# A hybrid encoder step on one core: mixer pairs interleaved over four PSUM banks, weight parts traced ahead, element-wise steps moved to ScalarE

## The chip, the core and the metric

The kernel runs on one core of a Trainium2 chip. The metric is device microseconds of one execution: 2014.56 us before the change, the median of three runs (2006.13 to 2015.11). Engines are named as the profile names them: PE is the matmul engine TensorE (PEld its weight loads), DVE is VectorE, ACT is ScalarE, POOL is GpSimd, and SP is the engine that issues most transfers.

## What is computed

One layer of a streaming encoder is applied to 576 tokens (512 of a prompt, 64 of a sample with caches), with 1024 channels, all in fp32:

- x + 1/2 SwiGLU(RMSNorm(x)), with a hidden width of 4096;
- plus a mixer: one input projection of RMSNorm(x) feeds three branches. Branch A is a Mamba-2 SSD scan (16 heads of 64, 4 groups, state 128, causal convolution of width 4, SiLU gate). Branch B is attention over a band of chunks (8 heads of 64, softmax with a bias by relative distance). Branch C is an mLSTM (4 heads of 128, exponential input gate, running maximum). Each branch is projected to 1024 channels, multiplied by a sigmoid gate of its own, summed, and projected again;
- plus a second half SwiGLU, and a final RMSNorm.

The outputs are the two results and the new states and caches.

## The kernel before

**Stages.** In order of time: the first SwiGLU (to about 595 us of the span), the plain products for the mixer's first two units (to 643), the mixer's pairs with the branches between them (643 to 1250), the merge of the branches with the output projection (its last matmul starts at 1422), the second SwiGLU and the final norm. Tokens lie on the free axis, channels on the 128 partitions.

**Split products.** Each fp32 weight tile is split into a high part `ph` (a cast on ACT, L268) and a low part `pl` (a subtraction on DVE, L269), and so are the activations (TH and TL). A product sums three matmuls per 128 rows, hi x hi, hi x lo and lo x hi (`product`, L563): 4 x 3 = 12 matmuls of 288 columns each.

**Seven products for eight.** Two output tiles of 128 channels are made together, as a 2 x 2 block product with seven sub-products, Winograd's form of Strassen's scheme. The seven are named X1 to X4, A11, A21, A22 after the weight block they take. X1 is the sum of two blocks, added up by an accumulating transfer from POOL (L445) into the tile `wx` (x12, which also holds X2). X3 and X4 are sums that POOL makes (`wy`, L456). In the mixer one such pair of output tiles is a call of `pair` (L466): it fetches the next pair's weights, splits all seven weight blocks of this pair behind the evacuations of the middle of the pair before it (`self.middle`, an `issue_after`), and issues the products in the order X1, X4, X2 of the pair before, X3, A21, A11, A22. Intermediate sums are copied from PSUM to `uv` tiles (L485, on ACT), and results leave through `emit` (L491 on ACT, L493 on DVE).

**PSUM.** Eight banks: in the mixer three for `acc`, two each for the tags `s` and `x`, one for `v`. A pair takes three `acc` banks, and the next pair starts one bank further on. `x` holds transpositions on PE (L769, L772, L814, L985, L1083, L1087), and in the mLSTM and SSD jobs one accumulation.

**Units and jobs.** The mixer works through twelve units: a0 to a3 (two attention heads each), m0 to m3 (one mLSTM head each), s0 to s3 (one SSD group each), in the order `a0 a1 m0 s0 a2 a3 s1 m1 s2 m2 s3 m3`. A unit's input tiles come from pairs (those of a0 and a1 from plain products ahead of the pairs), and then its job (`attn`, `ml`, `ssd`) is queued. A job is a Python generator: every product calls `tick` (L529), and each tick lets the first job of the queue trace its next step, or counts down a gap that the step asked for. Jobs run strictly one after another. Gate pairs (`merge_gates`, 12 in all) make the tanh inputs of the merge gates and store them to DRAM (`gs`). There are 23 unit pairs and 12 gate pairs, 35 x 7 = 245 products. After each unit's pairs comes one gate pair, and then the unit's job is queued. The last two units have two gate pairs each.

**Buffers.** Rings of tiles by tag: `g` 9, `t` 5, `P` 4, `uv` 3 in the mixer; `wr` 5, `wx` 2, `wy` 2, `ph` 6, `pl` 6 for weights. The tag `P` serves the attention scores (L834, L852), the mLSTM's decay matrix and the raw input of the SSD convolution (L1004).

**What sets the order.** A planner orders the instructions of every engine at build time: it prefers what was traced earlier, among what a simulated run of the program finds ready. The engines then run their queues strictly in that order.

## Time and profile before

| What | Value |
|---|---|
| Median of three runs | 2014.56 us (2006.13 to 2015.11) |
| The profiled execution | 2008.22 us, its span 2006.5 us |
| Mean granted TensorE clock | 0.981 |
| PE busy | 1938.0 us, 97% of the span |
| PE weight loads | 1868.3 us, 93% |
| DVE busy | 1376.9 us, 69% |
| ACT busy | 987.8 us, 49% |
| POOL busy | 637.0 us, 32% |

How to read the views. Groups of instructions: source line, engine, operation, output<-inputs, shape, count | busy us in total, mean ns of one | idle us of the engine just before them, and what ended it. Stretches: from:to, length, busy us (and count) of PE, PEld, DVE, ACT and POOL, then the granted clock, the busy share of the DMA engines and GB/s. Waits: who waited for whom, us in total, how many, the longest. Order of time: start, duration, engine, line, operation, and in brackets the idle time before it. A tile's name is the program's own, and a line can be that of a helper.

### The profile page before, as it was taken

The page shows a single profiled execution, that of the slowest core. Times are in us where ns is not written, and L with a number is a line of the kernel's source. Part 1 is how long each engine was busy: PE and PEld are TensorE (multiplying, and loading weights), DVE is VectorE, ACT ScalarE, POOL GpSimd, SP SyncE. Part 2 cuts the span into 40 slices and gives each one's busy share as a digit, 9 for nine tenths or more (in the row PEclk, how much of TensorE's full clock was granted, in tenths as well). Part 3 has the DMA queues.
Part 4 walks back from the last instruction along what each step waited for, and adds up shares of the span by engine and source line. Part 5 has one row for each costly group of instructions (what it writes and reads, how often), then busy time and mean ns, then how long its engine had stood idle before and what let it go on. Part 6 is the DMA issues. An engine that isn't in the chain of part 4 may idle for free. (4 is left out here: it accounts for less than half of the span.)

```text
span 2006.5 us, 37549 instructions
## 1 busy us (share of the span) xinstructions
PE 1938.0 (97%) x14177; PEld 1868.3 (93%) x14177; DVE 1376.9 (69%) x2475; ACT 987.8 (49%) x2153; POOL 637.0 (32%) x626
## 2 busy tenths in 40 slices
PE   9899999999999999998999898899999999999998
PEld 8899999999999768877888888899999999999998
DVE  8866656666678958777686766665786665666565
ACT  4545434534544556666574754333554443454454
POOL 5223313322202326423534354351142322223221
PEclk9899999999999979999999999899999999999999
DMA  6346445544643436753655567652234644464441
GB/s 195 82 129 165 120 127 148 144 116 125 166 135 102 137 98 152 206 149 95 189 149 166 157 167 209 223 173 80 79 110 122 158 133 121 131 164 121 122 117 63
DMA packets 126622, 278.18 MB, mean 139 GB/s; under 512 B 14032, under 2 KB 25936, under 8 KB 126440
## 3 DMA queue, kind: packets, MB, share of 16 engines
q1 hardware_dynamic: 100648, 201.74, 30.3%
q0 software_dynamic: 16304, 59.52, 16.4%
q10 hardware_dynamic: 9488, 14.52, 2.4%
q8 instruction: 112, 1.84, 0.4%
q14 instruction: 70, 0.57, 0.1%
HBM read 255.16 MB, written 20.56 MB: 137 GB/s over the span
## 5 line engine op out<-in xcount | busy, mean ns | idle before, releaser
L570 PE MATMUL acc<-TH,ph 128*128 128x288 f32 x2548 | 769.4, 302 | 15.6 <-ACT uv L485 5.2
L570 PE MATMUL acc<-TL,ph 128*128 128x288 f32 x2548 | 758.6, 298 | 3.4 <-DVE TL L269 3.4
L570 PE MATMUL acc<-TH,pl 128*128 128x288 f32 x2548 | 757.4, 298 | 2.1 <-DVE pl L269 2.0
L268 ACT CAST ph<-wr 128x512 fp32r<-128x512 f32 x495 | 306.0, 620 | 481.0 <-PE acc L570 209.1
L570 PEld LDWEIGHTS acc<-TH,ph 128*128 128x128 f32 x2548 | 481.8, 189 | 27.7 <-ACT uv L485 7.4
L570 PEld LDWEIGHTS acc<-TH,pl 128*128 128x128 f32 x2548 | 483.0, 190 | 8.6 <-issue 4.7
L570 PEld LDWEIGHTS acc<-TL,ph 128*128 128x128 f32 x2548 | 482.5, 189 | 6.8 <-DVE TL L269 3.6
L269 DVE TENSOR_TENSOR pl<-wr,ph 128x512 fp32r<-128x512 f32 x495 | 378.2, 766 | 125.1 <-ACT ph L268 115.6
L240 PE MATMUL acc<-YH,ph 128*128 128x320 f32 (+1 forms) x1536 | 453.3, 297 | 6.4 <-DVE y L1214 3.2
L240 PE MATMUL acc<-YL,ph 128*128 128x320 f32 (+1 forms) x1536 | 455.1, 297 | 2.6 <-DVE YL L319 2.1
L240 PE MATMUL acc<-YH,pl 128*128 128x320 f32 (+1 forms) x1536 | 452.3, 296 | 0.0
L240 PEld LDWEIGHTS acc<-YH,ph 128*128 128x128 f32 x1536 | 291.0, 190 | 7.8 <-DVE y L1214 3.7
L240 PEld LDWEIGHTS acc<-YL,ph 128*128 128x128 f32 x1536 | 292.1, 190 | 4.3 <-DVE YL L319 3.5
L240 PEld LDWEIGHTS acc<-YH,pl 128*128 128x128 f32 x1536 | 291.3, 190 | 0.0
L456 POOL TENSOR_TENSOR wy<-wx,wr 128x512 f32<-128x512 f32 x91 | 133.0, 1462 | 442.3 <-DVE pl L269 191.1
L445 POOL DMA_DIRECT2D wx<-in_sblk x91 | 80.6, 889 | 374.9 <-DMA wx<-in_sblk 165.0
L269 DVE TENSOR_TENSOR pl<-wx,ph 128x512 fp32r<-128x512 f32 x182 | 171.3, 941 | 36.3 <-ACT ph L268 33.5
L269 DVE TENSOR_TENSOR pl<-wy,ph 128x512 fp32r<-128x512 f32 x182 | 149.3, 830 | 50.5 <-ACT ph L268 50.4
L631 DVE SCALAR_TENSOR_TENSOR R<-acc,R 128x256 f32<-128x256 f32 (+1 forms) x256 | 116.1, 454 | 90.2 <-PE acc L240 86.9
L268 ACT CAST ph<-wy 128x512 fp32r<-128x512 f32 x182 | 112.4, 621 | 100.2 <-PE acc L240 63.0
L268 ACT CAST ph<-wx 128x512 fp32r<-128x512 f32 x182 | 112.7, 619 | 94.8 <-PE acc L570 63.3
L456 POOL TENSOR_TENSOR wy<-wy,wr 128x512 f32<-128x512 f32 x91 | 135.3, 1486 | 32.3 <-DMA wr<-in_sblk 16.2
(290 smaller groups left out, 2216.5 us busy)
## 6 DMA issues: line engine op xcount, KB each, us to landing
wr<-in_sblk SPq DMA_DIRECT2D x273, 256.0 KB, 2.8
wr<-in_wblk SPq DMA_DIRECT2D x222, 256.0 KB, 3.1
wx<-in_sblk SPq DMA_DIRECT2D x91, 512.0 KB, 4.0
wx<-in_sblk POOLq DMA_DIRECT2D x91, 512.0 KB, 5.7
gs<-g SPq DMA_DIRECT2D x24, 288.0 KB, 3.4
R<-scr_rows ACTq DMA_DIRECT2D x12, 576.0 KB, 5.6
y<-gs POOLq DMA_DIRECT2D x24, 288.0 KB, 3.5
y<-ys POOLq DMA_DIRECT2D x16, 288.0 KB, 3.6
```

What stands on the lines that cost most here:

```text
L240: nc.tensor.matmul(ps[:, :n], wt[:, wsl], xx[:, k0 + k, a:a + n], start=(k == 0 and i == 0), stop=(k == nk - 1 and i == 2))
L268: self.nc.scalar.copy(hi, src)
L269: self.nc.vector.tensor_tensor(lo, src, hi.bitcast(F32), op=ALU.subtract)
L445: nc.gpsimd.dma_start(x12, src[:, 1:3, :], accum_op=ALU.add)
L456: self.nc.gpsimd.tensor_tensor(o, one, two, op=ALU.add)
L570: self.nc.tensor.matmul(ps, wt[:, wsl], xx[:, kk, :], start=(start and kk == 0 and i == 0), stop=(kk == 3 and i == 2), skip_group_check=True)
L631: nc.vector.scalar_tensor_tensor(x[:, ot, sl], ps, 0.5, x[:, ot, sl], op0=ALU.mult, op1=ALU.add)
```

## The change

Five things change.

1. `pair` becomes `pairs`, which walks one list of products for the whole mixer. A round of pair n is X1(n), A22(n-1), X4(n), A11(n), X3(n), X2(n-1), A21(n), so that two pairs are always open. The banks are fixed: `acc0` and `acc3` in turn for the products that share a bank (X1, X3, A22, X2), `acc1` for X4 and A21, `acc2` for A11. There are four `acc` banks, and `x` has one bank instead of two.
2. A weight block's parts are no longer made for a whole pair at once: the parts of product i + 5 are traced ahead of product i. The `issue_after` on the middle of the pair is gone. `wx` has three buffers, `uv` four.
3. Three element-wise steps go to ACT: the softmax rescale (from DVE), the weighted values `wv` of the mLSTM (from POOL), and the weighted inputs `xw` of the SSD (two instructions on POOL become ten on ACT).
4. A unit's job is queued when X2 of its last pair has been issued, ahead of the gate pair and no longer behind it. The unit before last has no gate pair, and four gate pairs come after the last unit.
5. To make room, a pad is smaller, and the descriptor scratch of the transfers that POOL issues is 8192 bytes. The feed-forward units call the same `operand`, so that their two POOL additions are traced after two of the parts.

```diff
@@ -39,10 +40,13 @@
 FBUFS = {"P": 6, "g": 4}
-WBUFS = {"wr": 5, "wx": 2, "wy": 2, "ph": 6, "pl": 6}
+WBUFS = {"wr": 5, "wx": 3, "wy": 2, "ph": 6, "pl": 6}
 PAD = 2700
-PBUFS = {"s": 2, "x": 2, "v": 1}
+PBUFS = {"s": 2, "x": 1, "v": 1}
 NWARM = 14
+
+AHEAD = 5
+NGATES = {10: 0, 11: 4}
@@ -168,11 +171,8 @@
-    def pair_banks(self):
-
-        got = [self.bank()[:, :FH] for _ in range(3)]
-        self.bank_i += self.pair_step - 3
-        return got
+    def half_bank(self, i):
+        return self.acc.tile([128, 512], F32, name="acc", tag=f"acc{i}", bufs=1)[:, :FH]
@@ -449,7 +445,7 @@
-    def stationary(self, raw):
+    def operand(self, raw, t):
@@ -457,32 +453,34 @@
         x12 = raw["x12"]
-        x3 = add(x12[:, 0, :], raw[2])
-        x4 = add(x3, raw[3])
-        at = {self.T_X1: x12[:, 0, :], self.T_X2: x12[:, 1, :], self.T_X3: x3, self.T_X4: x4,
-              self.T_A11: raw[0], self.T_A22: raw[2], self.T_A21: raw[3]}
-        return {t: self.parts(at[t]) for t in (self.MUSE if self.mixer else self.FUSE)}
-
-    def pair(self, one, two, nxt):
-
-
-
-
-        nc = self.nc
-        ((name, c1), s1, put1), ((_, c2), s2, put2) = one, two
-        raw = self.fetched
-        if nxt:
-            self.fetched = self.fetch(nxt)
-        with ExitStack() as order:
-            for i in self.middle:
-                order.enter_context(self.tc.issue_after(i))
-            ops = self.stationary(raw)
-        pa, pc, pb = self.pair_banks()
+        if t in (self.T_X3, self.T_X4) and "x3" not in raw:
+            raw["x3"] = add(x12[:, 0, :], raw[2])
+            raw["x4"] = add(raw["x3"], raw[3])
+        return self.parts({self.T_X1: x12[:, 0, :], self.T_X2: x12[:, 1, :], self.T_X3: raw.get("x3"),
+                           self.T_X4: raw.get("x4"), self.T_A11: raw[0], self.T_A22: raw[2], self.T_A21: raw[3]}[t])
+
+    def pairs(self, seq):
+
+
+
+
+        nc = self.nc
+        uses = [(n - d, t) for n in range(len(seq) + 1) for d, t in (
+            (0, self.T_X1), (1, self.T_A22), (0, self.T_X4), (0, self.T_A11), (0, self.T_X3), (1, self.T_X2), (0, self.T_A21))
+            if 0 <= n - d < len(seq)]
+        raw, ops, st = {}, {}, {}
         H = (slice(0, FH), slice(FH, T))
+        def make(n, t):
+            for m in (n, n + 1):
+                if m < len(seq) and m not in raw:
+                    (((name, c1), _, _), ((_, c2), _, _)), _ = seq[m]
+                    raw[m] = self.fetch((name, c1, c2))
+            ops[n, t] = self.operand(raw[n], t)
+
         def tmp(ps, scale):
-            o = self.gp.tile([128, FH], F32, name="uv", tag="uv", bufs=3)
-            self.last = nc.scalar.activation(o, ps, AF.Copy, scale=scale).ins
+            o = self.gp.tile([128, FH], F32, name="uv", tag="uv", bufs=4)
+            nc.scalar.activation(o, ps, AF.Copy, scale=scale)
             return o
@@ -490,38 +488,42 @@
                     return
-                self.last = nc.vector.scalar_tensor_tensor(dst, ps[:, a:b], scale, other[:, a:b], op0=ALU.mult,
-                                                           op1=op).ins
+                nc.vector.scalar_tensor_tensor(dst, ps[:, a:b], scale, other[:, a:b], op0=ALU.mult, op1=op)
                 if func:
...
-        self.product(pa, ops, self.T_X1, True)
-        v = tmp(pa, s1)
-        self.product(pc, ops, self.T_X4, True)
-        m6 = tmp(pc, s2)
-        self.pair_end()
-        self.product(pa, ops, self.T_X3, False)
-        u = tmp(pa, s2)
-        self.middle = [self.last]
-        self.product(pc, ops, self.T_A21, False)
-        put2(1, H[1], emit(pc, s2, u, ALU.subtract))
-        self.middle.append(self.last)
-        self.product(pb, ops, self.T_A11, True)
-        put1(1, H[1], emit(pb, s1, v, ALU.add))
-        self.product(pa, ops, self.T_A22, False)
-        put2(0, H[0], emit(pa, -s2, m6, ALU.add))
-
-        def end():
-            self.product(pa, ops, self.T_X2, False)
-            put1(0, H[0], emit(pa, s1))
-        self.open_pair = end
-
-    def pair_end(self):
-
-        end, self.open_pair = self.open_pair, None
-        if end:
-            end()
+        for i, (n, t) in enumerate(uses):
+            for u in uses[(i + AHEAD if i else 0):i + AHEAD + 1]:
+                make(*u)
+            ((_, s1, put1), (_, s2, put2)), done = seq[n]
+            o = st.setdefault(n, {})
+            if t == self.T_X1:
+                o["a"] = self.half_bank(3 * (n % 2))
+            elif t == self.T_X4:
+                o["c"] = self.half_bank(1)
+            elif t == self.T_A11:
+                o["b"] = self.half_bank(2)
+            bank = {self.T_X4: "c", self.T_A21: "c", self.T_A11: "b"}.get(t, "a")
+            ps = o[bank]
+            self.product(ps, ops.pop((n, t)), t, t in (self.T_X1, self.T_X4, self.T_A11))
+            if t == self.T_X1:
+                o["v"] = tmp(ps, s1)
+            elif t == self.T_X4:
+                o["m6"] = tmp(ps, s2)
+            elif t == self.T_A11:
+                put1(1, H[1], emit(ps, s1, o["v"], ALU.add))
+            elif t == self.T_X3:
+                o["u"] = tmp(ps, s2)
+            elif t == self.T_A21:
+                put2(1, H[1], emit(ps, s2, o["u"], ALU.subtract))
+            elif t == self.T_A22:
+                put2(0, H[0], emit(ps, -s2, o["m6"], ALU.add))
+            else:
+                put1(0, H[0], emit(ps, s1))
+                if done:
+                    done()
+                del raw[n], st[n]
@@ -562,7 +564,7 @@
         self.tick()
-        hi, lo = ops[t]
+        hi, lo = ops
         th, tl = self.T[t]
@@ -573,31 +575,34 @@
         nc = self.nc
-        ops = self.stationary(self.fetch(desc))
-        pa, pb, pc = self.pair_banks()
+        raw = self.fetch(desc)
+
+        ops = {t: self.operand(raw, t) for t in (self.T_X1, self.T_A11, self.T_X3, self.T_X4, self.T_A22, self.T_A21,
+                                                 self.T_X2)}
+        pa, pb, pc = (self.bank()[:, :FH] for _ in range(3))
         e = lambda: self.P((128, FH))
         g = self.wp.tile([128, 2, FH], F32, name="g", tag="g", bufs=FBUFS["g"])
-        self.product(pa, ops, self.T_X1, True)
+        self.product(pa, ops[self.T_X1], self.T_X1, True)
...
@@ -802,7 +807,7 @@
             nc.vector.reciprocal(r[:, 0:1], total)
-            nc.vector.tensor_scalar(P[:, :nk], P[:, :nk], r[:, 0:1], None, op0=ALU.mult)
+            nc.scalar.activation(P[:, :nk], P[:, :nk], AF.Copy, scale=r[:, 0:1])
@@ -939,7 +944,7 @@
             wv = self.unit([128, 130], "wv", 2)
-            nc.gpsimd.tensor_scalar(wv[:n, :129], v1[:n, c, :], wc[:n, c:c + 1], 1.0, op0=ALU.mult, op1=ALU.mult)
+            nc.scalar.activation(wv[:n, :129], v1[:n, c, :], AF.Copy, scale=wc[:n, c:c + 1])
             pc = self.ps("s")
@@ -1087,10 +1092,10 @@
                                     self.TM[:64, 4:5, d0:d0 + 2].unsqueeze(3).broadcast_to([64, 1, 2, 64]), op=ALU.mult)
-            nc.gpsimd.tensor_tensor(h4(xw[:, 0:4, :]), h4(xd[:, 0:4, :]),
-                                    wd[:, 0:4, :].unsqueeze(3).broadcast_to([128, 4, 2, 64]), op=ALU.mult)
-            nc.gpsimd.tensor_tensor(h4(xw[:64, 4:5, :]), h4(xd[:64, 4:5, :]),
-                                    wd[:64, 4:5, :].unsqueeze(3).broadcast_to([64, 1, 2, 64]), op=ALU.mult)
+            for c, (a, n) in enumerate(CH):
+                for r in range(2):
+                    hs = slice(r * 64, (r + 1) * 64)
+                    nc.scalar.activation(xw[:n, c, hs], xd[:n, c, hs], AF.Copy, scale=wd[:n, c, r:r + 1])
@@ -1294,7 +1299,7 @@
             self.pbufs = PBUFS
-            self.banks, self.bank_i, self.pair_step = 3, 0, 1
+            self.banks, self.bank_i = 4, 0
             self.mixer = True
@@ -1316,7 +1321,7 @@
         with self.pools("m0", op=None, xp=None):
-            self.op.tile([128, 84], F32, name="pad")
+            self.op.tile([128, 8], F32, name="pad")
             self.XH, self.XL = self.pair_of(self.xp, [128, 8, T], ("XH", "XL"))
@@ -1335,12 +1340,15 @@
             self.ss = [na[:, a:a + n] for a, n in HALVES]
-            queue = lambda n: self.jobs.append(units[ORDER[n][0]][1](ORDER[n][1], got[ORDER[n]][1]))
+            def queue(n):
+                self.jobs.append(units[ORDER[n][0]][1](ORDER[n][1], got[ORDER[n]][1]))
+                if n == len(ORDER) - 2:
+                    self.jobs.append(self.ssd_norm())
             queue(0)
...
             self.side = self.gates(pre)
-
             seq = []
+            gates = iter(range(12))
             for n in range(2, len(ORDER)):
@@ -1350,18 +1358,9 @@
                 seq += [(tiles[j:j + 2], None) for j in range(0, len(tiles), 2)]
-                seq.append((self.merge_gates(n - 2), n))
-                if n - 2 >= len(ORDER) - 4:
-                    seq.append((self.merge_gates(n), None))
-            descs = [(one[0][0], one[0][1], two[0][1]) for (one, two), _ in seq] + [None]
-            self.fetched = self.fetch(descs[0])
-            for (tiles, n), nxt in zip(seq, descs[1:]):
-                self.pair(*tiles, nxt)
-                if n is not None:
-                    queue(n)
-                    if n == len(ORDER) - 2:
-                        self.jobs.append(self.ssd_norm())
-            self.pair_end()
+                seq[-1] = (seq[-1][0], partial(queue, n))
+                seq += [(self.merge_gates(next(gates)), None) for _ in range(NGATES.get(n, 1))]
+            self.pairs(seq)
             self.drain()
@@ -1446,7 +1445,7 @@
-    nc = bacc.Bacc("TRN2", target_bir_lowering=False, num_devices=1)
+    nc = bacc.Bacc("TRN2", target_bir_lowering=False, num_devices=1, dynamic_dma_scratch_size=8192)
     I = {k: nc.dram_tensor("in_" + k, s, F32, kind="ExternalInput").ap() for k, s in _INS.items()}
```

More of the change, by code (lines that the diff above doesn't have):

```diff
@@ L16 @@
 from contextlib import ExitStack, contextmanager, nullcontext
+from functools import partial
 import numpy as np
@@ L83, in __init__ @@
         self.b_i = 0
-        self.open_pair, self.middle = None, ()
         self.jobs, self.gap, self.side = deque(), 0, iter(())
@@ L130, in ffn_phase @@
             self.pbufs = {"x": 2}
-            self.banks, self.bank_i, self.pair_step = 6, 0, 3
+            self.banks, self.bank_i = 6, 0
             self.mixer = False
@@ L430 @@
     T_X3, T_A11, T_A21, T_X2, T_A22, T_X4, T_X1 = range(7)
-    FUSE = (T_X1, T_A11, T_X3, T_X4, T_A22, T_A21, T_X2)
-    MUSE = (T_X1, T_X4, T_X3, T_A21, T_A11, T_A22, T_X2)
     def fetch(self, desc):
@@ L575, in swiglu_unit @@
         nc = self.nc
-        ops = self.stationary(self.fetch(desc))
-        pa, pb, pc = self.pair_banks()
+        raw = self.fetch(desc)
+        ops = {t: self.operand(raw, t) for t in (self.T_X1, self.T_A11, self.T_X3, self.T_X4, self.T_A22, self.T_A21,
+                                                 self.T_X2)}
+        pa, pb, pc = (self.bank()[:, :FH] for _ in range(3))
         e = lambda: self.P((128, FH))
         g = self.wp.tile([128, 2, FH], F32, name="g", tag="g", bufs=FBUFS["g"])
-        self.product(pa, ops, self.T_X1, True)
+        self.product(pa, ops[self.T_X1], self.T_X1, True)
         v = e()
         nc.scalar.copy(v, pa)
-        self.product(pb, ops, self.T_A11, True)
+        self.product(pb, ops[self.T_A11], self.T_A11, True)
         nc.vector.tensor_tensor(g[:, 1, :], pb, v, op=ALU.add)
-        self.product(pa, ops, self.T_X3, False)
+        self.product(pa, ops[self.T_X3], self.T_X3, False)
         u = e()
         nc.scalar.copy(u, pa)
-        self.product(pc, ops, self.T_X4, True)
+        self.product(pc, ops[self.T_X4], self.T_X4, True)
         m6 = e()
         nc.scalar.copy(m6, pc)
-        self.product(pa, ops, self.T_A22, False)
+        self.product(pa, ops[self.T_A22], self.T_A22, False)
         s0 = e()
@@ L594, in swiglu_unit @@
         nc.scalar.activation(s0, s0, AF.Silu)
-        self.product(pc, ops, self.T_A21, False)
+        self.product(pc, ops[self.T_A21], self.T_A21, False)
         s1 = e()
@@ L599, in swiglu_unit @@
         nc.gpsimd.tensor_tensor(g[:, 1, :], g[:, 1, :], s1, op=ALU.mult)
-        self.product(pa, ops, self.T_X2, False)
+        self.product(pa, ops[self.T_X2], self.T_X2, False)
         nc.vector.tensor_tensor(g[:, 0, :], pa, s0, op=ALU.mult)
```

## The prediction

> **What bounds it now.** I read the engine totals first, then the engines by stretch, then the matmul engine's waits inside the mixer, then the order of time around the one long hole.
>
> ```profile
> span 2006.5 us, 37549 instructions
> PE 1938.0 (97%) x14177; PEld 1868.3 (93%) x14177; DVE 1376.9 (69%) x2475; ACT 987.8 (49%) x2153; POOL 637.0 (32%) x626
> ```
>
> The matmul engine (PE) is busy 97% of the span, so it sets the end, and only its idle time and its slow stretches can be won. The next view gives busy us of PE, weight load, VectorE, ScalarE and GpSimd by stretch, with the granted clock.
>
> ```profile
> 100.00:150.00 50.00, 50.00 (x378) 50.00 (x377) 31.27 (x53) 20.70 (x40) 13.12 (x11) 1.00 0.46 127
> 655.00:700.00 45.00, 42.72 (x271) 35.33 (x272) 44.61 (x100) 23.23 (x61) 12.97 (x12) 0.96 0.47 130
> 740.00:1000.00 260.00, 247.60 (x1803) 220.46 (x1802) 196.11 (x391) 159.44 (x412) 117.01 (x117) 0.99 0.58 156
> 1000.00:1247.00 247.00, 228.53 (x1650) 215.14 (x1649) 177.14 (x326) 148.36 (x381) 111.01 (x115) 0.97 0.60 166
> 1247.00:1296.00 49.00, 39.26 (x272) 37.53 (x271) 29.07 (x58) 16.99 (x39) 14.71 (x26) 0.93 0.74 235
> 1296.00:1480.00 184.00, 183.52 (x1364) 182.63 (x1363) 123.80 (x225) 75.81 (x146) 62.90 (x64) 0.99 0.33 105
> ```
>
> The feed-forward stretch at 100 runs without a hole: 50/378 = 0.132 us a matmul, 1.59 us a product of 12, 11.1 us a pair of 84. So the feed-forward parts have nothing to give, and their edits (a third wx buffer, the two GpSimd additions traced after two parts instead of ahead of all) count nothing: full PE work hides them, and if that cover failed, the cost would be about one GpSimd addition a unit (1.46 us, its row stands below). All the loss lies between 655 and 1296. These waits end inside the mixer's pairs (745 to 1250; us in total, times, longest) and, below the dots, at the step into the merge (1247 to 1300):
>
> ```profile
> PE ps_s L1117 <- POOL t L1090: 8.4, 3, 3.4
> PE ps_s L944 <- POOL wv L942: 5.2, 4, 2.0
> PE acc L570 <- ACT uv L485: 5.2, 7, 1.5
> PE acc L570 <- DVE pl L269: 2.0, 2, 1.2
> PE acc L570 <- DVE R L493: 1.9, 1, 1.9
> PE acc L570 <- DVE g L493: 1.6, 3, 0.8
> PE acc L570 <- DVE P L493: 1.3, 1, 1.3
> ...
> PE ps_x L955 <- DMA cs<-in_mc: 3.4, 1, 3.4
> PE acc L240 <- DVE y L1214: 3.2, 1, 3.2
> PE acc L240 <- ACT YH L268: 2.5, 1, 2.5
> ```
>
> The named waits in the pairs come to 25.6 us. One hole is larger and shows in no row of waits. In order of time, PE and then VectorE, with the stretch's totals:
>
> ```profile
> 707.96 0.29 PE L570 MATMUL acc<-TH,pl 128*128 128x288 f32 x1
> ...
> 738.86 0.40 PE L570 MATMUL acc<-TH,ph 128*128 128x288 f32 x1
> ...
> 737.50 0.16 DVE L851 TENSOR_TENSOR sm<-sm 128x1 f32<-128x1 f32 x1
> 737.58 0.88 DVE L493 SCALAR_TENSOR_TENSOR P<-acc,uv 128x224 f32<-128x224 f32 x3
> ...
> 708.10:738.80 30.70, 27.06 (x110) 13.63 (x107) 14.42 (x53) 16.51 (x59) 0.49 (x5) 0.61 0.29 78
> ```
>
> For 30.9 us no product runs. PE does one attention job alone, at a granted clock of 0.61. It ends when VectorE empties a bank into a P tile, right behind the job's last softmax step. The first SSD unit's convolution input and the attention scores share the four P buffers, and the job's last P is traced first.
>
> **The change, part by part.** Base: the profiled execution's 2008.2 us (span 2006.5 and 1.7 around it). The three timed runs have a median of 2014.56, from 2006.13 to 2015.11, so the base lies at their lower end.
>
> ```profile
> L1090 POOL TENSOR_TENSOR t<-t,wd 128x512 f32<-128x512 f32 x8 | 9.8, 1223 | 7.4 <-DVE t L1084 7.4
> L1092 POOL TENSOR_TENSOR t<-t,wd 64x128 f32<-64x128 f32 x8 | 7.7, 965 | 1.9 <-DVE t L1088 1.5 <-ACT sq L279 0.4
> L456 POOL TENSOR_TENSOR wy<-wx,wr 128x512 f32<-128x512 f32 x91 | 133.0, 1462 | 442.3 <-DVE pl L269 191.1 <-DMA wx<-in_sblk 93.4 <-DMA wr<-in_sblk 52.5
> L853 ACT ACTIVATE P<-ps_s,sm 128x64 f32<-128x64 f32 x4 | 1.2, 308 | 0.0
> L942 POOL TENSOR_SCALAR wv<-t,wc 128x129 f32<-128x129 f32 (+1 forms) x20 | 11.2, 620 | 12.6 <-ACT t L770 10.0 <-PE ps_s L944 2.6
> L1099 ACT ACTIVATE R<-R,TM 128x128 f32<-128x128 f32 (+1 forms) x80 | 25.4, 381 | 0.0
> L805 DVE TENSOR_SCALAR P<-P,sm 128x128 f32<-128x128 f32 (+4 forms) x36 | 15.8, 439 | 0.3
> L834 ACT ACTIVATE P<-ps_s,sm 128x128 f32<-128x128 f32 (+3 forms) x32 | 16.8, 525 | 7.2 <-DVE P L805 3.3 <-DVE sm L833 2.2 <-DVE TM L739 1.6
> L485 ACT ACTIVATE uv<-acc 128x288 f32<-128x288 f32 x105 | 42.4, 406 | 39.6 <-PE acc L570 34.2 <-DVE g L1021 3.9 <-DMA scr_rows<-R 1.4
> ```
>
> *xw to ScalarE.* Eight times, 1.22 + 0.97 = 2.2 us on GpSimd become ten activations 64 wide, 3.1 us at 0.308 each. But the first chunk is ready after two of them (0.6 us), and it no longer queues behind a 1.46 us addition. Of the 8.4 us I take back 6. Bounds: -8.4, or +7 if each set is late by the 0.9 us that it is longer.
>
> *wv to ScalarE.* 0.62 becomes about 0.38 us (nearest width, 128). The waits were 5.2 us; I take 4 back. Bounds: -5.2 and 0.
>
> *Softmax rescale to ScalarE.* 36 times, 0.44 us on VectorE becomes 0.53 on ScalarE (the exponential of the same widths), 0.09 x 36 = 3 us longer, in jobs that PE covers with products. VectorE gains 15.8 us. That counts where VectorE is the limit, 655 to 700 (44.61 of 45 us busy): one attention job there has ten rescales, 4.4 us. I take -3. Bounds: -4.4 and 0. The Trainium skill speaks against this move ("ScalarE: Activation LUTs", section "Rules for kernel authors"): multiplications belong on VectorE. Its formula for an activation with a pointer operand, 280 ns plus 0.833 per element, gives an estimate of 0.56 us at the mean width of 339, against 0.44 measured on VectorE; the trace agrees in direction, and by it the 3 us would be 4, off PE's path either way.
>
> *Interleaving and the fourth bank.* A product that reuses a bank now mostly has three products since the bank's last use instead of two: 4.8 us instead of 3.2 for the evacuation. The waits of this kind (uv, R, g, P) are 5.2 + 1.9 + 1.6 + 1.3 = 10.0; I take 7 back. But X1 of a pair now reuses the bank of X2 two pairs earlier with only A21 between, 1.59 us, against two products before. That can cost 35 times up to one evacuation (0.406 us), 14 us. I take 3, since one evacuation and a handoff fit into 1.59. Bounds: -10 and +14.
>
> *Parts five products ahead.* 5 x 1.59 = 8 us of lead for cast, subtraction and addition, in six buffers. The splits now precede the jobs' steps in preference. The waits on pl are 2.0 us: -2, bounds -2 and 0. Three wx buffers cover the longer life of x12, whose X2 part now comes a round later. The loads are as many as before and a pair ahead, on SP and GpSimd, but traced 5 products sooner, so on SP they may stand longer for a free wr buffer. Behind them stand the stores of gates, outputs and branch rows, for which only the rings of nine g and five t tiles wait. A load needs 2.8 us and a pair lasts 11.1, so I count 0.
>
> *One x bank instead of two.* Every transposition must now wait for the copy out of the one before it.
>
> ```profile
> L817 ACT COPY Q<-ps_x 128x512 f32<-128x512 f32 (+3 forms) x36 | 15.8, 440 | 20.6 <-PE ps_x L814 18.6 <-PE ps_v L866 1.6
> L770 ACT COPY t<-ps_x 128x512 f32<-128x512 f32 x16 | 9.2, 578 | 3.6 <-PE ps_x L769 3.6
> ```
>
> These 52 copies take 15.8 + 9.2 = 25 us, the upper bound, if PE stands through each. The lower bound is 0, if a product always fills in. Behind a transposition that waits, PE's queue holds products, and their banks. The planner places products there, so I take a quarter: +6.
>
> *Gate pairs at the end.* A job advances one step a product. Counting steps in the code, the last SSD job starts at product 208 instead of 210 of 245, so the last mLSTM job starts at 237 instead of 239: two products, 3.2 us, off the step into the merge, where the three waits quoted above are 9.1 us. I take -3. Bounds: -9.1 and 0. The four pairs give less cover than their number says, as the jobs run one after another and the last waits for the one before. They also hold two g tiles at a time of nine, beside four of the last mLSTM unit and up to three of the last SSD unit. A tile comes free when its store has landed, in 3.4 us; a pair lasts 11.1, so I count 0, and 4 x 3.4 = 14 us as the bound if each pair had to wait for one.
>
> ```profile
> wr<-in_sblk SPq DMA_DIRECT2D x273, 256.0 KB, 2.8
> gs<-g SPq DMA_DIRECT2D x24, 288.0 KB, 3.4
> ```
>
> *The long hole.* The second attention job's last P is traced at product 25 both before and after. The SSD input that waits for it, through A21 of the fourth pair, comes at product 25 before and 26 after, behind it again. So I count 0. Bounds: +6 (the copies of one job serialised), and -22 (the job's weight loads, 13.63 us at clock 0.61, are 8.3 at full clock; 30.7 - 8.3).
>
> The smaller descriptor scratch touches GpSimd's transfers, which show no wait of the kind: 0.
>
> Sum: -6 -4 -3 -7 +3 -2 +6 -3 = -16, so 2008.2 - 16 = **1992 us**. Its own range, from part of the bounds, is 1976 to 2004.
>
> **The rivals.** *The hole closes too.* For it: VectorE is relieved in the stretch before it, and half of the SSD inputs (A11) are now traced earlier, ahead of the last score tile. Against: the tracing order above. 1992 - 22 = 1970.
>
> *No net gain.* The pairs' waits move from GpSimd and the banks to the single x bank: the +6 becomes +22 of its 25. For it: 52 copies are all on ScalarE, where casts queue as well. 1992 + 16 = 2008.
>
> *Slower: ScalarE, in order, becomes the choke.* It takes 36 x 0.525 + 20 x 0.38 + 80 x 0.308 = 51 us more, where it is now busy (159.44 + 148.36)/507 = 61% from 740 to 1247. It also holds still, before each xw for its input (the 7.4 us in GpSimd's row) and before each rescale for VectorE's reciprocal:
>
> ```profile
> 733.16 0.20 ACT L834 ACTIVATION_READ_ACCUMULATOR P<-ps_s,sm 128x1 f32 x1
> ...
> 733.59 0.48 DVE L805 TENSOR_SCALAR P<-P,sm 128x512 f32<-128x512 f32 x1
> ```
>
> Here 733.59 - 733.36 = 0.23 us pass, 8 us in 36. Together 51 + 7 + 8 = 66 us, with casts and bank evacuations behind them. If 36 of these land on PE the time is 1992 + 36 = 2028. It decides from 16 on, where the gain is gone. Against: five products of lead cover most casts.
>
> **How the numbers follow.** Forecast 0.50, hole closes 0.15, no net gain 0.17, slower 0.18. About 0.5% is what a measurement of this kernel tells from no change: against the median, 2004.5 and 2024.6. Faster: nine tenths of the first and the second, 0.60. Same: the rest of the first and most of the third, 0.20. Slower: 0.20. The range 1955 to 2030 takes in the second and the fourth, and the bounds of hole and bank.
>
> **What would show it.** Right: the rows of PE waiting for GpSimd's t and wv are gone, uv's is under 3 us, VectorE has 15.8 us less; the hole near 708 is still over 20 us; a new row of PE ps_x waiting for ScalarE copies under 8 us. Wrong: new PE acc waits on ScalarE over 20 us, or ScalarE near full from 740 to 1247 (third rival); the hole gone, with more than 30 us won (first); a wait on x over 15 us (second).

## The result, and the profile after

| | Before | After |
|---|---|---|
| Median, the two timed in turn | 2011.51 us (2006.13 to 2015.11) | 1988.47 us (1985.05 to 1991.23) |
| Ratio, 95% interval | | 0.9887 [0.9854, 0.9919] |
| Profiled execution, its span | 2008.22, 2006.5 | 1985.05, 1983.3 |
| Granted clock, mean | 0.981 | 0.984 |
| Feed-forward 1, plain products (from the span's start) | 642.7 | 641.7 |
| Pairs, first product to last | 607.4 | 580.2 |
| From there to the last matmul of the output projection | 171.8 | 178.5 |
| From there to the end | 584.6 | 583.0 |

The median before is of four runs here: the three behind the 2014.56 above, and one more. Forecast 1992, measured 1988.5, profiled 1985. As a gain, 16 us were forecast and 23 came, by the medians and by the profiled executions alike. The total lies in the range; several of its terms are wrong, and they offset one another. The table's stages are bounded by the starts of matmuls in the traces. The gain is in the pairs, 27.2 us; 6.7 are given back in the step behind them, and the other stages differ by 1.0 and 1.6.

The engine totals of the kernel after:

```profile
PE 1922.6 (97%) x14177; PEld 1860.7 (94%) x14177; DVE 1358.8 (69%) x2439; ACT 1040.9 (52%) x2295; POOL 580.1 (29%) x590
```

VectorE has 18.1 us less, GpSimd 57 less, ScalarE 53 more. The moved steps explain only half of GpSimd's 57: they took 9.8 + 7.7 + 11.2 = 28.7 us. The rest is in steps that stayed and got shorter; the weight additions, for one, took 268.3 us before and 255.9 after. The stretch of the pairs by engine, before, and under it the matmuls of the products alone (from:to, length, then busy us and count of PE, weight load, VectorE, ScalarE and GpSimd; clock, DMA share, GB/s):

```profile
642.70:1250.10 607.40, 568.85 (x4005) 506.05 (x4004) 449.35 (x909) 364.86 (x953) 250.98 (x267) 0.96 0.57 155
642.70:1250.10 607.40, 445.93 (x2939) 403.94 (x2940) 0.96 0.57 155
```

The same after:

```profile
641.70:1221.90 580.20, 550.73 (x3972) 495.93 (x3970) 423.55 (x866) 409.02 (x1083) 213.28 (x225) 0.98 0.58 160
641.70:1221.90 580.20, 433.86 (x2940) 400.51 (x2940) 0.98 0.58 160
```

PE's idle time (length less busy) falls from 38.6 to 29.5 us, 9.1 of the 27.2. The other 18.1 is busy time: 12.1 in the same 2940 product matmuls (151.7 to 147.6 ns each), and 6.0 in the jobs' matmuls, some of which now run behind the last product. Counted in the two traces, the products are broken into by a job's matmuls 195 times before and 152 times after. At full clock the first product matmul behind a job's takes 0.22 us to the next one, the others 0.13, so this is about 4 of the 12.1. About 2 more are the clock: 51 product matmuls start at half clock before and 36 after. The rest stays open, as the profile models the ends of matmuls. The forecast looked for its gain in named waits. These are the waits inside the pairs, after:

```profile
PE acc L572 <- ACT uv L483: 8.4, 4, 4.4
PE ps_x L819 <- ACT Q L822: 4.9, 8, 1.5
PE ps_x L819 <- ACT P L810: 3.2, 1, 3.2
PE ps_s L1122 <- ACT st L1125: 3.0, 2, 1.8
PE acc L572 <- ACT ph L268: 2.1, 2, 1.1
PE ps_x L777 <- ACT t L775: 2.0, 2, 1.4
PE acc L572 <- DVE g L491: 1.7, 1, 1.7
...
PE ps_x L774 <- DVE t L778: 0.8, 1, 0.8
PE acc L572 <- DVE pl L269: 0.7, 1, 0.7
```

The rows of PE waiting for GpSimd (8.4 and 5.2 us before) are gone. The row of `uv` has grown from 5.2 to 8.4, where under 3 was forecast. The waits for copies out of the one `x` bank (Q, t) are 4.9 + 2.0 = 6.9 us for ScalarE and 1.2 for VectorE (0.8, and 0.4 in a row left out). In the row of `P` (L810) PE stands 3.2 us for a softmax rescale that now runs on ScalarE; before, it stood 2.0 for one on VectorE.

The long hole is still there, 22.1 us from 713.2 instead of 30.9 from 708.0. A new one of 12.8 us lies at 874.0. Both end as the old one did, when VectorE empties a bank into a P tile that an attention job has just given up (in order of time, after):

```profile
732.75 0.69 DVE L854 TENSOR_REDUCE sm<-ps_s 128x1 f32<-128x512 f32 x1
733.96 0.52 DVE L491 SCALAR_TENSOR_TENSOR P<-acc,uv 128x224 f32<-128x224 f32 x2 [0.52 <-PE ps_x L819]
...
884.57 0.50 DVE L491 SCALAR_TENSOR_TENSOR P<-acc,uv 128x224 f32<-128x224 f32 x2
```

### The profile page after: what moved, and what is told of

Its sections match the earlier page's. It is cut to its first block, busy times and chain, and to the rows that moved or that the text cites. A ratio compares the mean times of both kernels' runs of the same rounds, so it can differ in the third digit from the quotient of the medians.

```text
span 1983.3 us, 37588 instructions
## 1 busy us (share of the span) xinstructions
PE 1922.6 (97%) x14177; PEld 1860.7 (94%) x14177; DVE 1358.8 (69%) x2439; ACT 1040.9 (52%) x2295; POOL 580.1 (29%) x590
## 3 DMA queue, kind: packets, MB, share of 16 engines
q1 hardware_dynamic: 100648, 201.74, 30.9%
## 4 chain that ended last, share of the span: by engine, by line
PE 46%; ACT 2%; DMA 2%; issue 1%; POOL 0%; DVE 0%; ACTq 0%; POOLq 0%; DVEq 0%
PE acc L572 24%; PE acc L240 20%; DMA wx<-in_sblk 1%; DMA y<-ys 1%; DMA R<-scr_rows 1%; ACT R L1104 1%; ACT ph L268 0%; PE ps_s L1122 0%; PE ps_v L1144 0%; PE ps_x L1151 0%; POOL R L402 0%; PE ps_s L949 0%; ACT L1050 0%; ACT junk L977 0%; DMA ys<-g 0%
## 5 line engine op out<-in xcount | busy, mean ns | idle before, releaser
L269 DVE TENSOR_TENSOR pl<-wr,ph 128x512 fp32r<-128x512 f32 x495 | 384.5, 777 | 133.6 <-ACT ph L268 121.0
L452 POOL TENSOR_TENSOR wy<-wx,wr 128x512 f32<-128x512 f32 x91 | 127.6, 1403 | 331.7 <-DVE pl L269 179.0
L269 DVE TENSOR_TENSOR pl<-wy,ph 128x512 fp32r<-128x512 f32 x182 | 162.8, 894 | 83.0 <-ACT ph L268 78.6
L269 DVE TENSOR_TENSOR pl<-wx,ph 128x512 fp32r<-128x512 f32 x182 | 137.3, 754 | 42.7 <-ACT ph L268 39.4
L452 POOL TENSOR_TENSOR wy<-wy,wr 128x512 f32<-128x512 f32 x91 | 128.3, 1410 | 94.9 <-DVE pl L269 49.2
```

The lines of the kernel that those rows point to most:

```text
L269: self.nc.vector.tensor_tensor(lo, src, hi.bitcast(F32), op=ALU.subtract)
L452: self.nc.gpsimd.tensor_tensor(o, one, two, op=ALU.add)
```

## The experiments

Each was timed in turn with the kernel before (medians 2014.48, 2013.89, 2011.41 and 2013.76 us in four sets), and ratios are to it. Idle time of the pairs is read from their stretch, as above. A profile shows one execution, and executions of one kernel differ by some us: the profile of the kernel before took 2008.22 us, 3 to 6 under its four medians, those of `b_moves` (2019.24) and `b_x1` (2043.83) 3 and 6 over their own.

### The three moves, alone and taken back

`b_moves`: the kernel before, with only the softmax rescale, `wv` and `xw` on ScalarE.

```diff
-            nc.vector.tensor_scalar(P[:, :nk], P[:, :nk], r[:, 0:1], None, op0=ALU.mult)
+            nc.scalar.activation(P[:, :nk], P[:, :nk], AF.Copy, scale=r[:, 0:1])
...
-            nc.gpsimd.tensor_scalar(wv[:n, :129], v1[:n, c, :], wc[:n, c:c + 1], 1.0, op0=ALU.mult, op1=ALU.mult)
+            nc.scalar.activation(wv[:n, :129], v1[:n, c, :], AF.Copy, scale=wc[:n, c:c + 1])
...
+                    nc.scalar.activation(xw[:n, c, hs], xd[:n, c, hs], AF.Copy, scale=wd[:n, c, r:r + 1])
```

> The kernel before with the three element-wise moves to ScalarE alone (rescale, wv, xw). Theory, by the prediction's terms: PE's waits on GpSimd's t (8.4 us) and wv (5.2 us) go, 6 + 4 + 3 = 13 us won, ratio to before 0.9935. Rival: without the five products of lead the weight casts queue behind the moved steps on ScalarE, and new PE waits on ScalarE give the gain back: ratio 1.000 or above.

Measured: 2015.88 us, 1.0009 [0.9992, 1.0026]. No gain. The stretch of its pairs, and its first waits there:

```profile
642.00:1256.30 614.30, 568.79 (x4004) 509.54 (x4003) 433.36 (x874) 411.95 (x1093) 225.43 (x231) 0.96 0.56 153
```

```profile
PE acc L570 <- ACT uv L485: 12.8, 6, 3.9
PE acc L570 <- DVE pl L269: 4.8, 5, 1.6
```

The waits for GpSimd are gone, and PE's idle time is 45.5 us, not 38.6: what was taken from GpSimd came back as waits for ScalarE (`uv` 12.8 instead of 5.2) and for the weight parts (4.8 instead of 2.0). The 7 us more of idle time are no measure of a loss, as the two profiles differ by 11 us and the medians by 1.4; that the waits moved is what they show. That PE lacked a fourth `acc` bank to go on with is the likely reason, but four banks alone were not tried.

`a_nomoves`: the kernel after, with these three steps where they were (the diff above, reversed).

> The changed kernel with the three element-wise steps back on VectorE and GpSimd; interleaving, four banks, one x bank, parts ahead and gate placement stay. Theory: it loses the 13 us of the moves, ratio to before 0.995, with the waits on GpSimd's t and wv back. Rival: interleaving and the parts' lead make the whole gain, ratio 0.989 like the changed kernel.

Measured: 2005.55 us, 0.9965 [0.9947, 0.9982]. The products alone in its pairs, and two waits there:

```profile
642.10:1244.20 602.10, 437.89 (x2939) 402.58 (x2940) 0.97 0.57 156
```

```profile
PE ps_s L1122 <- POOL t L1095: 9.2, 4, 3.9
PE acc L572 <- DVE g L491: 8.8, 5, 3.1
```

So the rest of the change gains 7 us without the moves by the ratio, 9 by the medians (2014.48 to 2005.55). The moves gain 16 to 19 more on top of it, by the changed kernel's two ratios, 0.9887 and 0.9871 (`after_again`, below). They are worth nothing in the old structure and more than the forecast's 13 in the new. Which piece of the new structure they need, the order of products, the fourth bank or the place of the jobs, was not separated; a lead of five products instead of two is not it (`a_ahead2`, below).

`a_rsdve`: the kernel after, with the rescale alone back on VectorE.

> The changed kernel with the softmax rescale back on VectorE, wv and xw left on ScalarE. All three moves back together cost 18 us on the changed kernel (ratio 0.9965 against 0.987). Theory 1 (the prediction: VectorE is the limit in the attention stretches, so the rescale is worth 3 us of it): ratio 0.988 to 0.990. Theory 2 (the gain of the moves is all from the two that left GpSimd, whose additions hold them up by 11 us of waits): ratio 0.986 to 0.988, no difference that can be told. Theory 3 (ScalarE, which copies for the one x bank, is the scarcer engine in the attention jobs): faster, ratio under 0.985.

Measured: 1991.71 us, 0.9899 [0.9878, 0.9921]. By the changed kernel's two ratios, 0.9887 and 0.9871, the rescale's move is worth 2 to 6 us. The forecast's 3 fits, but the intervals overlap, so the size isn't settled.

What the moved steps cost on ScalarE, in the kernel after (groups; the second row is all rescales, the others are by shape):

```profile
L1098 ACT ACTIVATE t<-t,wd 128x64 f32<-128x64 f32 x64 | 16.1, 335 | 1.7 <-DVE t L1089 1.7
L810 ACT ACTIVATE P<-P,sm 128x128 f32<-128x128 f32 (+4 forms) x36 | 21.1, 586 | 8.4 <-DVE sm L809 4.3 <-DVE ps_s L837 3.4 <-PE ps_v L882 0.6
L810 ACT ACTIVATE P<-P,sm 128x512 f32<-128x512 f32 x8 | 5.8, 722 | 0.6 <-DVE sm L809 0.4
L947 ACT ACTIVATE wv<-t,wc 128x129 f32<-128x129 f32 x16 | 5.7, 398 | 0.0
```

The forecast had taken 308 and about 380 ns for the first and the last, and 525 for the mean rescale, from rows of like width. By the formula that the Trainium skill gives ("ScalarE: Activation LUTs", section "What ACT_TABLE_LOAD costs", 280 ns plus 0.833 per element where an operand is a pointer) a width of 64, 512 and 129 gives estimates of 333, 706 and 387 ns; the rows of these shapes (335, 722, 398) agree within 3%. Its advice against multiplications on ScalarE holds for the duration of one (36 rescales take 21.1 us here, 15.8 on VectorE before). For the whole kernel it isn't borne out: with the rescale back on VectorE the median is higher, though within overlapping intervals. The other two moves left GpSimd, and `wv` runs shorter for it (620 ns there).

### One bank for the transpositions

`b_x1`: the kernel before, with one `x` bank.

```diff
-PBUFS = {"s": 2, "x": 2, "v": 1}
+PBUFS = {"s": 2, "x": 1, "v": 1}
```

> The kernel before with one x bank instead of two, the freed bank left unused. Theory, by the prediction's term: +6 us, ratio 1.003, in waits of PE on copies out of x. Rival: the jobs' chains get longer and show at the mixer's end and in the long hole, where no product covers them: +15 us or more, ratio 1.0075.

Measured: 2037.69 us, 1.0131 [1.0107, 1.0155]: 23 us over its set's median, 26 by the ratio. In its pairs:

```profile
640.40:1281.20 640.80, 576.53 (x3980) 518.52 (x3979) 434.39 (x903) 377.03 (x957) 248.32 (x262) 0.93 0.54 149
```

```profile
PE acc L570 <- ACT uv L485: 12.7, 7, 4.8
...
PE ps_x L814 <- ACT Q L817: 3.1, 6, 0.7
```

This is the rival's price (22 of 25), not the forecast's 6. But the waits for the bank itself are small (3.1 us, and 2.2 in the like row of `t`). PE stands 64.3 us in the pairs instead of 38.6. The cost appears as late banks for the products (12.7), a lower clock, 0.93, and later jobs: the first transposition of the last SSD job comes behind 212 products instead of 203, that of the last mLSTM job behind 244 instead of 238 (product matmuls that start ahead of it, by 12). In the kernel after, the same bank shows 8.1 us of waits, and the whole new structure with this bank in it still gains 7 to 9. What a second bank would win there wasn't tried: beside four `acc` banks it would leave only one for `s`.

### The lead of the weight parts

`after_again` is the kernel after, unchanged, as the set's measure; `a_ahead2` traces parts two products ahead.

```diff
-AHEAD = 5
+AHEAD = 2
```

> The changed kernel itself once more, beside the three that follow. Expected: ratio to before 0.985 to 0.992, the interval of its first timing. If it is 0.985 or below, the kernel with the gate pairs two and two (0.9854) gained nothing; if it is near 0.989, that one gained about 6 us.

> The changed kernel with the parts traced 2 products ahead instead of 5. Theory: the lead is what lets ScalarE take the moved steps, since alone they gained nothing; with 2 products (3.2 us) the waits of PE on the weight parts (ph and pl, 3.2 us now) grow past 15 us and most of the gain is lost, ratio to before 0.998. Rival: the fourth bank and the interleaving give the slack, the lead is worth its 2 us of pl waits: ratio 0.990.

Measured: 1987.45 us, 0.9871 [0.9856, 0.9887], and 1986.88 us, 0.9863 [0.9848, 0.9878]. No difference: two products of lead do what five do. Making all parts of a pair at once, as before, was not tried in the new structure.

### The end of the pairs

`a_gates`: two gate pairs behind each of the last two units, instead of four behind the last.

```diff
-NGATES = {10: 0, 11: 4}
+NGATES = {10: 2, 11: 2}
```

> The changed kernel with two gate pairs behind each of the last two units, as the kernel before has them, instead of none and four. Theory of the prediction: the placement is worth at most 3 us, so 0 to 3 us slower than the changed kernel, ratio to before 0.989 to 0.990. Rival: the stretch from the last product to the end of the merge grew by 6.7 us with the change because of the placement; then this kernel gets these back, ratio 0.9855.

Measured: 1983.44 us, 0.9854 [0.9833, 0.9874]; the step behind the pairs takes 174.1 us instead of 178.5, and the pairs 584.7 instead of 580.2. By the changed kernel's two ratios that is 3 to 7 us faster, but the intervals overlap, and in the profiles the two stages cancel (spans 1983.2 and 1983.3), so a gain isn't shown.

`a_norm_s`: the totals of the SSD norm go to a bank of the tag `s`; its transpositions stay in `x`.

```diff
         for (a, n), acc in zip(HALVES, self.ss):
-            pt = self.ps("x")
+            pt = self.ps("s")
             self.total([acc], n, pt)
```

> The changed kernel with the totals of the last SSD norm in a bank of the s pair instead of x. Theory: the norm's chain through the single x bank (1207 to 1223) holds the last mLSTM job back to after the last product; with the totals elsewhere it starts some 3 to 4 us sooner, 2 to 4 us won, ratio to before 0.987. Rival: the job waits for its turn in the order of jobs and not for the bank: no change, 0.989.

Measured: 1980.85 us, 0.9833 [0.9817, 0.9850], 7 us under `after_again` of its set, with intervals apart; the step behind the pairs takes 170.8 us instead of 178.5. In order of time on PE, the norm's last steps and the first step of the last mLSTM job in the kernel after:

```profile
1207.17 0.50 PE L294 MATMUL ps_x<-ones,sumsq 128*128 128x1 f32 x4
1211.72 0.61 PE L310 MATMUL ps_x<-ident,sm 128*128 128x128 f32 x4
1215.36 0.71 PE L294 MATMUL ps_x<-ones,sumsq 128*128 128x1 f32 x6
1219.43 0.97 PE L310 MATMUL ps_x<-ident,sm 128*128 128x128 f32 x6
...
1223.22 0.66 PE L774 MATMUL ps_x<-ident,g 128*128 128x128 f32 x4 [1.03 <-ACT rs L1175]
```

and with the totals in `s`:

```profile
1207.47 0.50 PE L294 MATMUL ps_s<-ones,sumsq 128*128 128x1 f32 x4
1208.44 0.71 PE L294 MATMUL ps_s<-ones,sumsq 128*128 128x1 f32 x6
1211.54 0.61 PE L310 MATMUL ps_x<-ident,sm 128*128 128x128 f32 x4
1215.36 0.97 PE L310 MATMUL ps_x<-ident,sm 128*128 128x128 f32 x6
1219.43 0.60 PE L774 MATMUL ps_x<-ident,g 128*128 128x128 f32 x4
```

With one `x` bank the norm's four steps stand in a chain of 12.3 us, each behind the one before; with the second total elsewhere, the job starts 3.8 us earlier and still beside products, whose last matmul starts at 1223.3. In the kernel after it starts behind the last (1221.9), and no product is left to fill PE's waits:

```profile
1222.00:1240.00 18.00, 10.78 (x61) 9.47 (x60) 5.79 (x11) 8.19 (x20) 6.71 (x10) 0.72 0.88 285
```

Of 18 us, 7.2 are idle, and the clock falls to 0.72. The same place with the totals in `s`:

```profile
1223.30:1240.00 16.70, 12.87 (x83) 11.50 (x82) 7.12 (x17) 8.02 (x26) 4.17 (x8) 0.90 0.97 320
```

`a_best`: both edits together.

> The changed kernel with two edits together: two gate pairs behind each of the last two units instead of four behind the last, and the totals of the SSD norm in a bank of the tag s instead of the one x bank. Alone they won 4 us (ratio 0.9854) and 7 us (0.9833) on the changed kernel's 0.987. Theory 1 (two separate causes: the norm's chain through the one x bank, and the place of the gate pairs): the gains add, ratio about 0.981 to 0.982, the merge's stretch from the last product of the pairs to the last of its own at or under 168 us. Theory 2 (one cause, the last mLSTM job starting late, which either edit removes): no more than the better one, ratio 0.983 to 0.985, that stretch about 171 us.

Measured: 1983.41 us, 0.9856 [0.9831, 0.9880]. The gains don't add. But the step behind the pairs is 176.6 us, over what either theory gave, though the job starts at 1217.2, the earliest of the four. In its trace the waits at the start of the merge are 4.9 us for `YH` and 4.7 for `y`, against 2.8 and 3.3 in `a_norm_s`, and the clock from 1223 to 1240 is 0.73, against 0.90. Why these inputs come later wasn't settled, so whether there is one cause or two stays open. `a_norm_s` has the lowest median of all versions.

### The hole

`a_P6`: six P buffers instead of four.

```diff
-BUFS = {"g": 9, "t": 5, "P": 4, "Q": 2, "bias": 2}
+BUFS = {"g": 9, "t": 5, "P": 6, "Q": 2, "bias": 2}
```

> The changed kernel with six P tiles in the mixer instead of four. Theory: the two holes without products (22.1 us from 713, 12.8 us from 874) come from the SSD convolution's raw inputs waiting for P tiles that the attention jobs hold; with six they shrink to under 6 us each, 15 to 22 us won, ratio to before 0.978 to 0.982. Rival: the holes are the length of the attention jobs' own chains, or move to the next short ring: ratio 0.989 as now, holes as long.

Measured: 1993.09 us, 0.9898 [0.9883, 0.9912], 6 us slower than `after_again`, with intervals that just touch. The first hole shrinks to 16.2 us, and the second grows from 12.8 to 22.0. The holes are not the whole of it: of the 12.6 us between the two profiled spans (1983.5 and 1996.1) 8.0 are in the step behind the pairs, where the last job starts 6.5 us behind the last product.

`a_raw2`: four P buffers, and a ring of two for the raw inputs of the SSD convolution alone.

```diff
-                    box["raw"] = raw = self.P((128, 582))
+                    box["raw"] = raw = self.fp.tile([128, 582], F32, name="raw", tag="raw", bufs=2)
```

> The changed kernel with a ring of its own, two buffers, for the raw inputs of the SSD convolution, so that they no longer share the four P buffers with the attention scores. In the changed kernel two long stretches hold no product, 22.1 us from 713 and 12.8 us from 874, and both end when VectorE empties a bank into such a raw tile, right behind a softmax step of an attention job. Theory 1 (the shared ring sets both holes): both shrink to under 6 us each, and the time falls by 12 to 25 us (not the whole 35, since the attention job's work on the matmul engine must still be done), ratio to the kernel before 0.974 to 0.981. Theory 2 (the attention job is a chain of single steps through the one x bank, and products are ordered behind it whatever is free): the holes stay within 3 us of 22 and 13 and the ratio within 0.985 to 0.990. With six P buffers for all, the first hole shrank to 16.2 us and the second grew to 22.0, which fits a shared ring whose order alone decides.

Measured: 2016.96 us, 1.0026 [1.0010, 1.0043]. Where the hole was, PE is now full, but the pairs take 600.7 us instead of 580.2:

```profile
641.50:1242.20 600.70, 555.52 (x3952) 500.28 (x3950) 416.92 (x863) 417.07 (x1087) 212.75 (x222) 0.97 0.55 153
713.20:741.00 27.80, 27.80 (x208) 25.32 (x208) 20.88 (x46) 17.51 (x53) 6.65 (x5) 1.00 0.55 144
```

So the shared ring does set the hole, and yet the hole's end wins nothing: other stretches without products come (7.6 and 10.1 us between 759 and 778, 7.8 at 852, 8.6 at 1143), and idle time is 45.2 us. The ring of two is a limit of its own, too: the products' waits for banks and weight parts are 24.4 us in these pairs, 12.9 in the kernel after, and 3.0 of the 24.4 are for a raw tile.

`a_raw3uv3`: three such buffers, and three `uv` buffers to make room.

```diff
-                    box["raw"] = raw = self.P((128, 582))
+                    box["raw"] = raw = self.fp.tile([128, 582], F32, name="raw", tag="raw", bufs=3)
...
-            o = self.gp.tile([128, FH], F32, name="uv", tag="uv", bufs=4)
+            o = self.gp.tile([128, FH], F32, name="uv", tag="uv", bufs=3)
```

> As the ring of two for the raw convolution inputs, but with three buffers (and, to make room, three uv buffers instead of four). With two, no stretch without products was left from 713 to 741, but new ones came (759 to 778, 852 to 860, 1143 to 1152), two of them with a raw tile late: by the interleaved order A11 of the next pair is emptied into a third raw tile before X2 of this pair has filled one of the first two. Theory 1 (the two buffers were the new wait, and the shared ring was the cost): the new stretches go as well, the pairs take under 570 us instead of 580.2, ratio to the kernel before 0.974 to 0.982. Theory 2 (the attention job's work on the matmul engine is only moved: products that no longer wait run ahead, and the jobs, one step a product, pile up later): stretches without products come elsewhere, above 25 us in all, ratio 0.985 or above.

Measured: 2031.19 us, 1.0091 [1.0072, 1.0110], slower again; the pairs take 616.0 us. Its waits:

```profile
PE ps_x L777 <- ACT t L775: 9.4, 4, 3.6
...
PE ps_s L833 <- ACT P L839: 6.3, 5, 2.5
PE acc L572 <- ACT uv L483: 5.2, 5, 2.7
```

The waits that grow most are those inside the jobs, such as those for the `x` bank's copies (9.4) and the softmax (6.3): all their rows come to 33.0 us in the pairs, from 16.5. Those of products for banks and weight parts grow less, from 12.9 to 20.1, and the row of `uv` falls from 8.4 to 5.2. That fits the second theory: products that no longer stand still run ahead, and the jobs, a step for each product, come late with less to cover them. The `uv` ring was changed with it, so its share isn't separated.

## Why the forecast was right, and where it was not

**Total:** 1992 against 1988.5, inside its own range of 1976 to 2004. The likeliest case, a small gain with the hole in place, came. But the gain was 23, not 16, and the sum was put together from terms of which few hold alone. That their errors offset one another is luck:

| Term | Forecast | What the runs showed |
|---|---|---|
| xw, wv and rescale on ScalarE | -6, -4, -3 | 0 in the old structure, -16 to -19 in the new |
| Interleaving and fourth bank, less X1's reuse | -4 | these rows, over all the pairs: 11.7 us before, 10.1 after |
| Parts five ahead | -2 | 0 against two ahead |
| One `x` bank | +6 | 8.1 us of waits in the new structure; +23 to +26 in the old |
| Gate pairs at the end | -3 | the step behind the pairs grew by 6.7, for another reason |
| The long hole | 0 | 30.9 to 22.1, and a new one of 12.8 |

**The moves.** The mechanism held: the two rows of GpSimd are gone, VectorE has 18.1 us less (15.8 forecast for the rescale; other rows of VectorE changed as well). The step that failed is to add them as terms of their own. Each was costed from a row of waits, as if the rest stayed; in the old structure the work on ScalarE came back as waits for evacuations (`b_moves`), in the new one it didn't. A slip without effect: an attention job has nine rescales (36 in four jobs), not ten.

**Interleaving.** "I take 7 back" of the waits for evacuations failed. The forecast's rows began at 745; over all the pairs of the kernel before, the one of `g` is

```profile
PE acc L570 <- DVE g L493: 3.3, 4, 1.8
```

so these rows are 5.2 + 3.3 + 1.9 + 1.3 = 11.7 us before and `uv` 8.4 + g 1.7 = 10.1 after: 1.6 less, not 7. The room of a fourth bank is not seen here. That it is what lets the moves win is likely, and not shown. The products' own busy time is 8.0 us less already without the moves (445.9 to 437.9) and 12.1 less with them. No term of the sum was for that; about 6 of the 12.1 have a source above.

**Parts ahead.** The row of pl fell from 2.0 to 0.7 us and a row of ph came (2.1). A lead of five products instead of two wasn't what mattered.

**The `x` bank.** In the new structure the quarter of 25 us (6, "under 8") fits the waits, 6.9 us for ScalarE's copies and 1.2 for VectorE's. In the old it is 23 to 26, at its upper bound of 25, with few waits for the bank: that bound counted copies PE stands through, not the jobs that come later and the clock that falls. So "no net gain" by this bank was not far off: without the moves the gain is 7 to 9 us.

**Gate pairs.** The step that this term was to shorten by 3 us grew by 6.7. The forecast counted steps by product and let the last mLSTM job start at product 237 instead of 239. Before, in order of time, it started here:

```profile
1234.91 0.66 PE L769 MATMUL ps_x<-ident,g 128*128 128x128 f32 x4
```

That is behind 238 products, as counted, and 15 us ahead of the last one (1250.1); after, it is 1.3 us behind the last (1221.9). What was overlooked is what the one `x` bank does to the jobs ahead, as its term priced only copies. In the kernel after, the last SSD job's first transposition comes behind 213 products instead of 203, and the norm's first total behind 238 instead of 233. The norm's own chain through that bank then adds two more, and these `a_norm_s` takes back. `b_x1` shows that the bank does it: with nothing else changed, the two jobs come behind 212 and 244 products. The place of the gate pairs alone isn't shown to cost (`a_gates`). Over the fourteen profiles, the step takes 170.8 to 176.6 us where the job starts ahead of the last product, and 178.0 to 187.3 where it starts behind it.

**The hole.** That it stays, for the order of tracing, was right, and the rival that closes it didn't come. That closing it would win up to 22 us was not borne out: with a ring of its own for the inputs the kernel is some 30 and 43 us slower than the change (`a_raw2`, `a_raw3uv3`, by the ratios), though each of these rings brings a limit of its own. A likely reason, not a shown one, is that the matmuls of the job in the hole have to run somewhere, and there they disturb no product.

**The slower rival** didn't come: ScalarE is busy 409 of 580 us, 70% in the pairs, and PE's `acc` waits for it are 8.4 + 2.1 = 10.5 us, under the 20 that would have shown it.

## What to carry to other kernels

A row of waits gives the price of a wait only while the rest stays: moving work off an engine won nothing here until the order of the products and their banks were changed as well, and then more than the rows said. A stretch in which one job runs alone need not be its length in loss: a ring that closed it here made the kernel slower, so try it before counting on it. And when two banks become one, follow every chain that uses them to the end of the stage: the jobs come later, and there nothing is left to cover them.

## What the runs showed that was not expected

The length of a hole goes with the clock. The old hole by stretches of 5 us, the last of 1 us (the third column from the right is the clock):

```profile
710.00:715.00 5.00, 2.63 (x6) 1.06 (x6) 2.01 (x10) 2.53 (x10) 0.00 (x0) 0.76 0.83 208
715.00:720.00 5.00, 5.00 (x30) 2.89 (x29) 2.15 (x9) 1.82 (x7) 0.00 (x0) 0.50 0.51 177
...
730.00:735.00 5.00, 5.00 (x18) 2.46 (x17) 3.06 (x9) 1.31 (x5) 0.00 (x0) 0.50 0.00 0
...
737.00:738.00 1.00, 0.70 (x6) 0.36 (x7) 0.93 (x5) 0.87 (x3) 0.00 (x0) 1.00 0.00 0
```

and the two holes of the kernel after:

```profile
715.00:720.00 5.00, 3.27 (x31) 1.85 (x30) 2.06 (x8) 2.43 (x6) 0.00 (x0) 1.00 0.79 218
720.00:725.00 5.00, 3.51 (x7) 1.27 (x8) 1.12 (x7) 3.67 (x17) 0.00 (x0) 0.58 0.17 65
...
880.00:885.00 5.00, 3.92 (x43) 2.83 (x43) 1.40 (x8) 3.31 (x8) 0.00 (x0) 1.00 0.30 84
```

The old hole runs at half clock from 712.6 to 736.5, behind PE's first long waits in it. The new one at 713 runs at full clock to about 721 and then near half. The one at 874 keeps full clock throughout and lasts 12.8 us, as it does at full clock in `after_again`, `a_ahead2`, `a_gates`, `a_norm_s` and `a_best`. In `a_P6` the clock falls to 0.50 at 867, ahead of the same place (871), and it lasts 22.0. A pair of score matmuls takes 2.07 us in the one state and 1.12 in the other:

```profile
722.76 2.07 PE L833 MATMUL ps_s<-g 64*128 64x512 f32 x2
...
867.77 1.12 PE L833 MATMUL ps_s<-g 64*128 64x512 f32 x2
```

The Trainium skill ("TensorE: Matmul & The Clock Gate", section "What's actually happening") says that the clock halves behind an idle window of about 3.4 us and comes back after a busy one. The fall fits that roughly: ahead of it PE stands for 0.83 and 2.52 us between 708.4 and 712.4, 3.35 us in all, with four transpositions between the two:

```profile
709.19 0.66 PE L814 MATMUL ps_x<-ident,P 128*128 128x128 f32 x4 [0.83 <-DVE TM L739]
712.37 1.03 PE L828 MATMUL ps_s<-g 64*128 64x256 f32 x2 [2.52 <-ACT P L834]
```

The return doesn't, by the busy time as the profile models it: from 715 to 735 PE is shown busy throughout, at 0.50. The clock comes back at 736.5, still among the job's matmuls, 2.4 us ahead of the first product (738.86).
